# Eight sums and differences of w_out_b's weights, on GpSimd instead of VectorE

## The chip, the cores and the metric

The kernel runs on one core of one Trainium2 chip. The metric is the device time of one execution in microseconds; the time before is the median of three runs. The engines that matter here: TensorE (PE in the profile) multiplies, VectorE (DVE) and ScalarE (ACT) do elementwise work, GpSimd (POOL) does elementwise work and issues some DMAs, SyncE (SP) issues most DMAs. Each engine works through its own list of instructions in order; semaphores make an instruction wait for others.

## The reference

One inference step of a hybrid decoder layer, for a prompt of 1024 tokens and eight samples of one token (1032 columns together), model width 1024, all in float32. Cut to what matters:

```
proj = h @ w_in                       # h: normalised, modulated input
hA, cA, bA, zA, qkv, zB, beta, alpha, gA, gB = split(proj)
yA = ((bA * conv3(cA * hA)) * silu(zA)) @ w_out_a
o  = rmsnorm(gated_delta(qkv, beta, alpha)) * silu(zB)
yB = o @ w_out_b                      # (1032 x 1024) @ (1024 x 1024)
merged = sigmoid(gA) * yA + sigmoid(gB) * yB
y = x + gate * rmsnorm(merged @ w_o)
```

## The kernel before

The large matrix products are made from operands split in two: a float32 tile is cast to a TensorE format (hi, on ScalarE), the rest is taken by a subtraction (lo, on VectorE), and three matmuls hi*hi, hi*lo, lo*hi are summed in PSUM. A weight tile of 128 x 1024 becomes `whi` (ScalarE) and `wlo` (VectorE); each name has two buffers, so a new `whi` waits until TensorE has finished with the pair two units earlier.

The run has stages. After a startup, `run` makes the q, k, v, z and gate columns of `w_in` and, beside them, the gated delta rule of eight heads. Then `products` makes the four column blocks h, c, b, z of branch A (eight groups t of them), and `products_b` makes yB. Then `run` makes the products with `w_out_a`, and a tail those with `w_o`.

`products` and `products_b` use a scheme of seven products in place of eight (Strassen's, in Winograd's form). The matrix of weights is cut into quarters a11, a12, a21, a22, and four new quarters are made of them: s = a21 + a22, a21' = a11 - a21, a11' = s - a11, a12' = a12 - a11'. The seven products P1, P2, P6, P7, P4, P5, P3 (in this order) use a11, a12, a11', a21', a22, s, a12'. For yB there are two column groups g = 0, 1, and a unit is one product of one group: P1 of group 0 (P1.0), P1.1, P2.0, P2.1, P6.0 and so on. A unit is 48 matmuls.

`weight_load` (from line 1454) loads the raw quarters with SyncE into tiles named `wr`, in the order a11, a12, a21, a22, each for both groups; a load waits for a free tile. `weight_gen` (from line 1470) makes `whi` and `wlo` of one unit after another, and behind those of P2 the four new quarters of its group: s into a tile of its own, `wsum`, the others in place over the raw tiles. So a21' must wait for s (which reads a21), a11' for a21', for s and for P1's `wlo` (which reads a11), and a12' for a11' and P2's `wlo`. There are eight instructions of 128 x 1024 float32 for yB: two named `wsum<-wr`, two `wr<-wsum,wr`, four `wr<-wr`. The same four are made for each of the eight groups t of branch A.

`yblock_gen` (from line 1531) brings the moving operands of yB. For P1, P2 and P3 SyncE loads rows (`yraw<-yBsc`) that ScalarE and VectorE split into `thi` and `tlo`. For P6, P7, P4 and P5 ready-made halves were parked in DRAM (`txs`) by `park_gen`, and GpSimd issues their loads: four products x two pairs of rows x two parts, 16 DMAs. `finish_group` ends a group of branch A with elementwise work on tiles named `acc`; for the last group this falls into the first units of yB. `evacuate` adds a finished product into its tiles from PSUM, on VectorE, but for P1, which ScalarE copies.

The order of the work comes from strands (generators) that `slot` and `force` step through beside the matmuls, by the clocks of a planner, `Sched`. `Paced` charges each instruction to its engine's clock: a two-input VectorE instruction 66 ns + elements/0.96 (1133 ns for 1024), a GpSimd one 100 ns + elements/1.2 (953 ns for 1024). The framework below places the instructions anew on each engine; in the trace, sums stand ahead of products that the code writes before them.

Nearly all instructions carry the line of the helper that records them (L129), so the views are read by tile names.

Of the kernel before, what the change touches and what calls it, by code (L numbers as in the profile page):

```python
# [12 lines left out]
ALU = mybir.AluOpType  # L13
# [155 lines left out]
def hybrid_step(  # L169
# [9 lines left out]
    V, A, PE, GP, SY = (Paced(e, n, sched) for e, n in (  # L179
        (nc.vector, "V"), (nc.scalar, "A"), (nc.tensor, "PE"), (nc.gpsimd, "GP"), (nc.sync, "SY")))  # L180
# [12 lines left out]
    def tt(out, a, b, op):  # L193
        V.tensor_tensor(out=out, in0=a, in1=b, op=op)
# [495 lines left out]
    def when(*conds):  # L690
        while not all(c() for c in conds):
            yield
# [777 lines left out]
    def weight_gen(raw):  # L1470

        sums = {}
        for n, (key, p, g) in enumerate(UNITS):
            a11, a12, a21, a22 = ((key, o, hf, g) for o in range(2) for hf in range(2))
            src = {"P1": a11, "P2": a12, "P6": a11, "P7": a21, "P4": a22, "P5": None, "P3": a12}[p]
            yield from when(lambda: unit[0] >= n - 1, lambda: src is None or src in raw)
            hi_ = wpool.tile([P, NK, P], F32R, tag="whi", name="whi", bufs=2)
            lo_ = wpool.tile([P, NK, P], F32R, tag="wlo", name="wlo", bufs=2)
            hi, lo = (v.rearrange("p k c -> p (k c)") for v in (hi_, lo_))
            v = raw[src] if src else sums.pop(g)  # L1480
            A.copy(out=hi, in_=v)
            yield
            tt(lo, v, hi.bitcast(F32), ALU.subtract)
            made[key, p, g] = (hi_, lo_)
            yield
            if p == "P2":
                yield from when(lambda: a22 in raw and a21 in raw)
                s_ = wpool.tile([P, NK, P], F32, tag="wraw", name="wsum", bufs=2)
                s_ = sums[g] = s_.rearrange("p k c -> p (k c)")
                tt(s_, raw[a21], raw[a22], ALU.add)  # L1490
                yield
                tt(raw[a21], raw[a11], raw[a21], ALU.subtract)
                tt(raw[a11], s_, raw[a11], ALU.subtract)
                yield
                tt(raw[a12], raw[a12], raw[a11], ALU.subtract)
            elif p in ("P6", "P7", "P4", "P3"):
                T4.give(raw.pop(src))

# [238 lines left out]
    def to_products():  # L1737
        drain_bg()
        T4.free = [i for i in T4.free if i[0] is not bp]
        bp.release()  # L1740
        T4.extend(alloc("m", "left"), "sl", NSL, NT)
        EARLY.extend(("gate", "wr", "qa", "qb", "q1"))
        raw = {}
        for g in (weight_load(raw), weight_gen(raw), block_gen()):
            start(g)
# [136 lines left out]
    for j in range(9):  # L1882
# [7 lines left out]
        for half in range(2):  # L1890
# [20 lines left out]
            gt = gtp if i < 8 else gts  # L1911
# [5 lines left out]
        for half in range(2):  # L1917
            hs = slice(half * 512, (half + 1) * 512)
            stt(yt[:n, hs], yt[:n, hs], r, xr[:n, hs], ALU.mult, ALU.add)
            out = y_prompt[0, i * P:(i + 1) * P, hs] if i < 8 else y_sample[:, 0, hs]  # L1920
# [39 lines left out]
```

## Time and profile before

| what | value |
|---|---|
| median of 3 runs | 1376.41 us (1374.74 to 1377.12) |
| the profiled execution's own time | 1375.67 us |
| its span | 1373.2 us |
| mean granted TensorE clock | 0.997 |
| ScalarE, VectorE busy | 666.2 us (49%), 969.6 us (71%) |
| DMA moved | 165.99 MB, mean 121 GB/s |
| products of yB | units from 1088.9 us to about 1174 us |

Times in the views are microseconds from the start of the span. A row of the view in order of time gives start, duration, engine, operation, written tile, read tiles, shape and count; a bracket gives the idle time of the engine just before and what ended it. Durations of neighbours overlap a little, since an engine takes its next instruction before the last has drained; what one costs its engine is read from start to start. The chain that ended last is followed back from the last instruction, at each step to what released it. Matmul ends are modelled. Profiled time and span differ by 2.5 us, which lie around the span.

### The profile page before, as it was taken

The numbers are of one execution on the slowest core, as the hardware profiler recorded it, in microseconds if no ns is written. First come the engines' busy times: TensorE is split into PE (matmuls) and PEld (weight loads), VectorE is DVE, ScalarE is ACT, GpSimd is POOL, SyncE is SP. The second block draws the span as 40 slices with busy tenths as digits, with TensorE's granted clock in tenths as the row PEclk, the third lists the DMA queues.
The fourth block names the chain that finished last, engine by engine and source line by source line (L and its number), as shares of the span: only waits on it lengthen the run. The fifth ranks groups of instructions, "written<-read, shape, count | busy, mean of one in ns | idle before, by whom it ended". The sixth has DMA issues, their size and how long they took to land.

```text
span 1373.2 us, 26429 instructions
## 1 busy us (share of the span) xinstructions
PE 1342.7 (98%) x10257; PEld 1278.0 (93%) x10257; DVE 969.6 (71%) x2495; ACT 666.2 (49%) x1554; POOL 46.3 (3%) x98
## 2 busy tenths in 40 slices
PE   5999999999999999999999999999999999999997
PEld 2799999999999999999998999999999999999786
DVE  4677877686969576695755999777777777754553
ACT  5586685576757575564543543222333354431221
POOL 1000010000001000000000000000000300000000
PEclk9999999999999999999999999999999999999999
DMA  9433333333343234333431654422232956652221
GB/s 318 134 112 97 97 101 85 86 110 88 93 106 99 64 99 116 84 100 88 140 102 53 223 191 154 124 78 72 68 98 84 280 181 218 229 168 71 83 96 46
DMA packets 184927, 165.99 MB, mean 121 GB/s; under 512 B 33709, under 2 KB 158366, under 8 KB 184794
## 3 DMA queue, kind: packets, MB, share of 16 engines
q1 hardware_dynamic: 180216, 155.71, 37.3%
q0 software_dynamic: 4384, 8.52, 2.1%
q8 instruction: 81, 1.33, 0.4%
q14 instruction: 44, 0.36, 0.1%
q10 hardware_dynamic: 202, 0.08, 0.0%
HBM read 127.59 MB, written 36.91 MB: 120 GB/s over the span
## 4 chain that ended last, share of the span: by engine, by line
PE 84%; DVE 7%; ACT 4%; DMA 3%; issue 1%; SPq 0%; DVEq 0%; ACTq 0%
PE pm_t L129 58%; PE pa_t L129 24%; PE pb L129 3%; DVE kq L129 2%; DVE wlo L129 1%; ACT junk L129 1%; DMA xs<-in_x_prompt_dram 1%; DVE Ttmp L129 1%; DVE Ts L129 1%; DMA Ts<-sT 1%; DMA wr<-in_w_out_b_dram 1%; ACT whi L129 0%; SPq L129 0%; ACT DB L129 0%; DVE S L129 0%
## 5 line engine op out<-in xcount | busy, mean ns | idle before, releaser
L129 PE MATMUL pm_t<-xh,whi 128*128 128x344 f32 (+1 forms) x1384 | 453.0, 327 | 0.4 <-DVE ban L129 0.4
L129 PE MATMUL pm_t<-xh,wlo 128*128 128x344 f32 (+1 forms) x1384 | 434.0, 314 | 0.0
L129 PE MATMUL pm_t<-xl,whi 128*128 128x344 f32 (+1 forms) x1384 | 433.9, 313 | 0.0
L129 PEld LDWEIGHTS pm_t<-xh,whi 128*128 128x128 f32 x1384 | 261.1, 189 | 3.5 <-issue 1.2
L129 PEld LDWEIGHTS pm_t<-xl,whi 128*128 128x128 f32 x1384 | 261.1, 189 | 0.1
L129 PEld LDWEIGHTS pm_t<-xh,wlo 128*128 128x128 f32 x1384 | 260.4, 188 | 0.1
L129 ACT CAST whi<-wr 128x1024 fp32r<-128x1024 f32 x60 | 63.0, 1050 | 138.3 <-PE pa_t L129 61.7
L129 ACT CAST whi<-wraw 128x512 fp32r<-128x512 f32 x112 | 68.4, 626 | 61.4 <-PE pm_t L129 50.0
L129 DVE TENSOR_TENSOR wlo<-wraw,whi 128x512 fp32r<-128x512 f32 x112 | 75.8, 686 | 27.1 <-ACT whi L129 26.3
L129 PE MATMUL pm_t<-thi,wlo 128*128 128x258 f32 x304 | 86.7, 285 | 2.5 <-DVE wlo L129 2.5
L129 PE MATMUL pm_t<-tlo,whi 128*128 128x258 f32 x304 | 86.6, 285 | 0.0
L129 PE MATMUL pm_t<-thi,whi 128*128 128x258 f32 x304 | 86.4, 284 | 0.0
L129 PE MATMUL pa_t<-tlo,whi 128*128 128x258 f32 x304 | 85.9, 283 | 0.0
L129 PE MATMUL pa_t<-thi,wlo 128*128 128x258 f32 x304 | 85.8, 282 | 0.0
L129 PE MATMUL pa_t<-thi,whi 128*128 128x258 f32 x304 | 85.7, 282 | 0.0
L129 DVE TENSOR_TENSOR wlo<-wr,whi 128x1024 fp32r<-128x1024 f32 x60 | 73.2, 1220 | 11.3 <-ACT whi L129 11.0
L129 PE MATMUL pa_t<-xh,whi 128*128 128x258 f32 x256 | 72.4, 283 | 0.0
L129 PE MATMUL pa_t<-xl,whi 128*128 128x258 f32 x256 | 72.4, 283 | 0.0
L129 PE MATMUL pa_t<-xh,wlo 128*128 128x258 f32 x256 | 72.2, 282 | 0.0
L129 DVE SCALAR_TENSOR_TENSOR kq<-raw,vecs,kq 128x528 f32<-128x528 f32 x96 | 70.2, 759 | 1.1 <-ACT kq L129 1.1
L129 ACT ACT_TABLE_LOAD x42 | 53.9, 1283 | 27.1 <-DVE kq L129 12.8
L129 PE MATMUL pm_t<-yhi,wlo 128*128 128x344 f32 x192 | 61.4, 320 | 0.0
(377 smaller groups left out, 2954.3 us busy)
## 6 DMA issues: line engine op xcount, KB each, us to landing
wraw<-in_w_in_dram SPq DMA_DIRECT2D x48, 512.0 KB
wr<-in_w_in_dram SPq DMA_DIRECT2D x64, 256.0 KB
aw<-in_ada_w_dram SPq DMA_DIRECT2D x16, 512.0 KB
gBsc<-gate SPq DMA_DIRECT2D x8, 516.0 KB
gAsc<-gate SPq DMA_DIRECT2D x8, 516.0 KB
txs<-phi SPq DMA_DIRECT2D x8, 516.0 KB
txs<-plo SPq DMA_DIRECT2D x8, 516.0 KB
yAsc<-acc SPq DMA_DIRECT2D x8, 516.0 KB
```

The lines of the kernel that those rows point to most:

```text
L129: r = f(*args, **kw)
```

## The change

For the key "B", that is the weights of w_out_b, the four instructions that make the new quarters of a group are issued on GpSimd; for the eight groups of branch A they stay on VectorE. The instructions, their operands and their place in the code are the same. Nothing else is edited; the planner charges them to GpSimd's clock.

```diff
                 s_ = wpool.tile([P, NK, P], F32, tag="wraw", name="wsum", bufs=2)
                 s_ = sums[g] = s_.rearrange("p k c -> p (k c)")
-                tt(s_, raw[a21], raw[a22], ALU.add)
-                yield
-                tt(raw[a21], raw[a11], raw[a21], ALU.subtract)
-                tt(raw[a11], s_, raw[a11], ALU.subtract)
-                yield
-                tt(raw[a12], raw[a12], raw[a11], ALU.subtract)
+                gt = tt if key != "B" else lambda o, a, b, op: GP.tensor_tensor(out=o, in0=a, in1=b, op=op)
+                gt(s_, raw[a21], raw[a22], ALU.add)
+                yield
+                gt(raw[a21], raw[a11], raw[a21], ALU.subtract)
+                gt(raw[a11], s_, raw[a11], ALU.subtract)
+                yield
+                gt(raw[a12], raw[a12], raw[a11], ALU.subtract)
```

## The prediction

> **What bounds the kernel now.** I read the page first, then the chain that ended last around the products of yB, then TensorE's and VectorE's instructions at the one break in that chain. (P1.0, P1.1, P2.0 and so on are product and column group g of the yB units; a11, a12, a21, a22 are their raw weights; s is the tile wsum.)
>
> ```profile
> span 1373.2 us, 26429 instructions
> PE 1342.7 (98%) x10257; PEld 1278.0 (93%) x10257; DVE 969.6 (71%) x2495; ACT 666.2 (49%) x1554; POOL 46.3 (3%) x98
> ```
>
> TensorE is busy 98% of the span and GpSimd 3%. Time off VectorE pays only where TensorE waits for VectorE. The chain shows one such place near the change (start us, us, what):
>
> ```profile
> 1077.49 1.06 ACT whi L129
> 1078.58 1.24 DVE wlo L129
> ...
> 1079.83 0.37 SPq L129
> ...
> 1080.25 8.46 DMA wr<-in_w_out_b_dram
> ...
> 1088.73 0.04 DVE wsum L129
> ...
> 1091.82 7.31 PE pm_t L129 x46
> 1099.12 5.72 PE pa_t L129 x48
> 1104.84 5.74 PE pm_t L129 x48
> 1110.58 5.75 PE pa_t L129 x48
> ...
> 1180.79 184.57 PE pm_t L129 x974
> ```
>
> To the right of 1091.82 the chain is TensorE alone to 1365, one unit of 48 matmuls every 5.75 us in the products of yB. To the left it leaves TensorE: a load of w_out_b takes 8.46 us, and a sum (wsum) starts when it lands. TensorE in order of time at that place:
>
> ```profile
> 1088.94 0.28 PE L129 MATMUL pm_t<-thi,whi 128*128 128x258 f32 x1
> 1089.06 0.28 PE L129 MATMUL pm_t<-tlo,whi 128*128 128x258 f32 x1
> 1091.82 0.58 PE L129 MATMUL pm_t<-thi,wlo 128*128 128x258 f32 x1 [2.48 <-DVE wlo L129]
> 1092.19 0.42 PE L129 MATMUL pm_t<-thi,whi 128*128 128x258 f32 x1
> ...
> 1095.21 0.31 PE L129 MATMUL pm_t<-thi,wlo 128*128 128x258 f32 x1
> ```
>
> P1.0 starts at 1088.94, issues two matmuls 0.12 us apart, and then stands until wlo, the low part of its weights. After that it runs at about half speed for 3.4 us; the view by stretches gives the granted clock (third figure from the end of a row, 0.59 and 1.00; before it busy time and instructions of each engine):
>
> ```profile
> 1092.00:1096.00 4.00, 4.00 (x22) 4.00 (x23) 4.00 (x9) 1.26 (x2) 2.46 (x4) 0.59 1.22 353
> 1096.00:1110.00 14.00, 14.00 (x120) 14.00 (x119) 13.22 (x15) 8.82 (x21) 0.00 (x0) 1.00 0.96 311
> ```
>
> Why wlo was late is in VectorE's and ScalarE's order of time (the bracket is the idle time before the instruction and what ended it):
>
> ```profile
> 1083.25 1.05 ACT L129 CAST whi<-wr 128x1024 fp32r<-128x1024 f32 x1 [4.71 <-PE pm_t L129]
> ```
> ```profile
> 1081.92 0.76 DVE L129 TENSOR_TENSOR acc<-pm_t,acc 128x258 f32<-128x258 f32 x2 [0.67 <-PE pm_t L129]
> 1088.73 1.22 DVE L129 TENSOR_TENSOR wsum<-wr 128x1024 f32<-128x1024 f32 x1 [6.05 <-DMA wr<-in_w_out_b_dram]
> 1089.88 0.75 DVE L129 TENSOR_TENSOR acc<-pm_t,acc 128x258 f32<-128x258 f32 x2
> 1090.55 1.22 DVE L129 TENSOR_TENSOR wlo<-wr,whi 128x1024 fp32r<-128x1024 f32 x1
> ...
> 1103.79 1.22 DVE L129 TENSOR_TENSOR wr<-wr 128x1024 f32<-128x1024 f32 x1
> 1104.92 1.22 DVE L129 TENSOR_TENSOR wr<-wsum,wr 128x1024 f32<-128x1024 f32 x1
> ...
> 1108.06 1.22 DVE L129 TENSOR_TENSOR wlo<-wr,whi 128x1024 fp32r<-128x1024 f32 x1 [0.78 <-ACT whi L129]
> ```
>
> whi of P1.0 was ready at 1084.3. Its wlo needs nothing else, but on VectorE it stands behind wsum of group 1, which waits 6.05 us for the last raw tile (a22 of group 1). The sum itself is used only by P5, many units later. An early, unneeded instruction holds up a late, needed one.
>
> **The change part by part.** *What leaves VectorE.* Eight instructions; between 1074 and 1112 us the view by tile lists exactly these:
>
> ```profile
> L129 DVE TENSOR_TENSOR wr<-wr x4: 1212/1216/1217, 1076.8 to 1109.5; 128x1024 f32<-128x1024 f32 x4
> L129 DVE TENSOR_TENSOR wsum<-wr x2: 1211/1218/1224, 1075.3 to 1088.7; 128x1024 f32<-128x1024 f32 x2
> L129 DVE TENSOR_TENSOR wr<-wsum,wr x2: 1214/1215/1216, 1092.3 to 1104.9; 128x1024 f32<-128x1024 f32 x2
> ```
>
> One costs VectorE 1.13 us, by start to start (1103.79 to 1104.92): 8 x 1.13 = 9.0 us. By itself this is worth nothing, since TensorE is the bound. What pays is the wait that leaves with wsum: VectorE no longer idles until 1088.73. wlo of P1.0 can follow its cast and the two evacuations queued before it: 1084.3 + 0.7 + 1.2, about 1086.2, which is 2.7 us before P1.0 starts.
>
> *The gain.* The third matmul of P1.0 would start 0.12 us after the second, at 1089.18 instead of 1091.82: 2.64 us. From 1091.82 to 1095.21 there are 16 intervals; at 0.12 us they take 1.92 instead of 3.39: 1.47 us. I take the half clock as the consequence of the break, as it is granted 0.59 there and 1.00 behind it. Together **4.1 us**. Nothing later in the chain is there to give it back: up to 1365 it holds only matmuls.
>
> *What GpSimd takes on.* No two-input arithmetic on GpSimd stands in the trace. The nearest rows are its copies (min/median/max in ns), and one of them beside VectorE:
>
> ```profile
> L129 POOL COPY raw<-hist_q x24: 205/208/2813, 63.6 to 578.1; 128x24 f32<-128x24 f32 x24
> ```
> ```profile
> L129 POOL COPY Ts<-Ti x8: 402/403/1152, 118.1 to 642.4; 128x256 f32<-128x256 f32 x8
> ```
> ```profile
> 187.69 2.81 POOL L129 COPY raw<-hist_q 128x24 f32<-128x24 f32 x1 [15.27 <-DVE kq L129]
> ```
> ```profile
> 187.49 0.67 DVE L129 TENSOR_TENSOR wlo<-wraw,whi 128x512 fp32r<-128x512 f32 x1
> 188.09 1.21 DVE L129 TENSOR_TENSOR kq<-kq,gcB 128x1024 f32<-128x1024 f32 x1
> 189.23 1.21 DVE L129 TENSOR_TENSOR DB<-DA,m_strict 128x1024 f32<-128x1024 f32 x1
> ```
>
> The undisturbed copies give 0.85 ns an element ((402 - 205) / 232), so a 1024-element copy would take 1.05 us: the lower bound. A second input read one after the other adds 0.87: **1.92 us**, my value, as it is the copy rows' own slope. Eight separate 256-element copies, 3.2 us, are the upper bound. The Trainium skill's GPSIMD Engine Reference, section 3.1 (Elementwise, side-by-side cycle accounting), gives 4497 ns for a two-input add of 2048 elements; an estimate of half, 2.25 us, lies inside these bounds.
>
> The copy at 187.69 takes 2.81 us instead of 0.21 and ends at 190.50, just as VectorE's three back-to-back two-input instructions end (189.23 + 1.21 = 190.44). So the two engines shut each other out for something. The trace shows GpSimd waiting, up to 2.6 us; whether VectorE waits for a long GpSimd instruction no row here can show, since GpSimd's own ones are too short. I bound it by 0 and by the whole GpSimd instruction. The Trainium skill's SBUF — State Buffer, section "Who interferes with whom", says that a VectorE instruction with two SBUF inputs and a GpSimd instruction that reads SBUF contend for an exclusive lock, and that whoever starts first holds it for the whole instruction. By that rule VectorE would wait; the stretched copy agrees with its other half.
>
> *What this does to VectorE.* Before, five of the eight sums run from 1088.73 up to wlo of P2.1 (1108.06), and that wlo ends 1.3 us before its unit (1109.3 against 1110.58): the tightest deadline. After, VectorE is free 5.3 us earlier (1083.4 instead of 1088.7) and TensorE 4.1 us earlier, a head start of 1.2 us. If each of the five kept VectorE shut out for all its 1.92 us, the lag would be 5 x (1.92 - 1.13) = 4.0 us, against 1.3 + 1.2 = 2.5 of room: wlo 1.5 us late. If half of that time falls on idle time or on evacuations, whose one input is in PSUM, the lag is 2.0 or less and nothing is late. VectorE has evacuations in every unit and no longer has the sums, so I take the half: cost **0**, bounds 0 and 5 x (3.2 - 1.13) - 2.5 = 7.9 us.
>
> *GpSimd's queue.* It also issues the loads of the parked blocks:
>
> ```profile
> 1089.51 0.71 POOL L129 DMA_DIRECT2D tlo<-txs  x1 [9.53 <-PE pa_t L129]
> ```
> ```profile
> thi<-txs POOLq DMA_DIRECT2D x8, 516.0 KB, 6.7
> ```
>
> Sums and these issues now stand in one line. A load put behind wsum of group 1 leaves up to 1.9 us after the tile's landing at 1088.7 and still lands some 7 us later, about 1098; the first block needed is P6's, loaded first, by unit four (1088.94 + 4 x 5.75 = 1111.9). Cost 0; cover gone if an issue slips by over 10 us. The other way round, sums behind the issues: seven more of 0.71 us after 1089.51 end near 1094.5; the sums s and a11' that P6.0's cast needs by 1106.2 (when P2.1 starts and a weight buffer is free) come second there, 1094.5 + 2 x (1.92 + 2.6) = 1103.5. Covered by 2.7 us. The planner charges GpSimd 953 ns for such an instruction and VectorE 1133, so the strands behind may be placed differently. I cannot price that from the trace; it widens the range.
>
> **The sum.** The profiled execution took 1375.67 us (span 1373.2 and 2.5 around it): 1375.67 - 4.1 = 1371.6. The median of the three runs lies 0.74 above it, so on that level the forecast is 1376.41 - 4.1 = **1372.3 us**.
>
> **The rivals.** *Eaten by the shared access.* Up to five GpSimd sums keep VectorE out for all their time; wlo of P2.1 is 1.5 us late, and with a fresh half-clock stretch of 1.5 us the kernel takes 1372.3 + 3.0 = 1375.3: no change. For it: VectorE is busy through 13.22 of 14 us at 1096 to 1110. Against: GpSimd is the one seen waiting. With the skill's price of 2.25 us in the same sum, wlo would be 3.1 us late and the time 1376.9.
>
> *The wait stays.* Another early instruction, waiting for the same loads, is placed before wlo of P1.0, or the raw tile comes later: 1376.4. For it: VectorE's order in the trace is not the code's (wsum ran ahead of a product that the code writes earlier), so it is newly made. Against: the other instructions in reach, evacuations and finish_group, follow TensorE and not a load.
>
> *Slower: GpSimd holds VectorE out.* The same place, wlo of P2.1, with a dearer instruction. Lateness is 5 x (p - 1.13) - 2.5, and 1.5 for the clock; it exceeds the gain of 4.1 and 0.2% (2.75) from p = 2.7 us on. At the upper bound of 3.2: 1372.3 + 7.9 + 1.5 = 1381.7. For it: the copy rows are single-input and say little of two inputs; against: their slope is far below, and TensorE would have to catch all five.
>
> **How the numbers follow.** A measurement of this kernel can tell about 0.2% (2.75 us) from no change: faster is below 1373.66, slower above 1379.16. Forecast, full gain or nearly: 50%, its own range 1370.8 to 1373.6. Eaten 18%, the wait stays 10%: 28% within 0.2%. Slower 22%. The range runs from 1370.8 (the forecast less 1.5 for the spread of runs, 1374.74 to 1377.12 before) up to 1380, leaving out the dearest of the slower cases, some 15%, and a few per cent below.
>
> **What would show it.** Right: no wait for wlo at P1.0, no stretch with a clock near 0.59 behind it, the eight sums on GpSimd near 1.9 us where VectorE is quiet, and wlo of P2.1 ahead of its unit. VectorE's two-input instructions of 128x1024 should stay at 1.2 us if it is not shut out; at 2 to 3 us they show the lock. Wrong: a new wait for wlo between P1.1 and P6.1, for whi behind a late a11', or for a parked block; or the DMA wait found again on VectorE before P1.0. A GpSimd sum above 2.7 us on its own would overturn the forecast.

## The result and the profile after

The changed kernel takes **1385.01 us** (median of six runs, 1382.53 to 1387.8) against 1375.68 us for the kernel before in six runs of its own (1374.56 to 1377.12). The ratio is **1.0067, interval 1.0053 to 1.0081**: 9.3 us slower. The forecast was 1372.3 us, and the time lies above its range, which ended at 1380.

The top of the page after, span and busy times:

```profile
span 1383.5 us, 26449 instructions
PE 1346.2 (97%) x10257; PEld 1279.7 (93%) x10257; DVE 973.5 (70%) x2487; ACT 665.8 (48%) x1554; POOL 66.5 (5%) x106
```

VectorE has eight instructions fewer (2487 for 2495), and yet its busy time has gone up, from 969.6 to 973.5 us. Eight instructions of 1.2 us left, and something else grew by more than they took. That is the first sign of where to look.

TensorE in order of time; the view shows no other wait of over 0.3 us from 1087 to the end:

```profile
1106.40 0.58 PE L129 MATMUL pm_t<-thi,wlo 128*128 128x258 f32 x1 [5.04 <-DVE wlo L129]
```
```profile
1121.58 0.39 PE L129 MATMUL pm_t<-thi,whi 128*128 128x258 f32 x1 [2.30 <-ACT whi L129]
1122.84 0.39 PE L129 MATMUL pm_t<-thi,wlo 128*128 128x258 f32 x1 [0.75 <-DVE wlo L129]
```

The wait of 2.48 us at P1.0 is gone. In its place stand 5.04 us at P2.0 (for VectorE) and 2.30 + 0.75 us at P6.0 (for ScalarE, then VectorE). Counting 48 matmuls to a unit gives each unit's start in both traces, and the shift of after against before tells what each place costs:

| unit | before, us | after, us | shift, us | step, us |
|---|---|---|---|---|
| P1.0 | 1088.94 | 1089.37 | +0.43 | |
| P1.1 | 1098.96 | 1095.16 | -3.80 | -4.23: the old wait and its half clock |
| P2.0 | 1104.68 | 1100.96 | -3.72 | +0.08 |
| P2.1 | 1110.42 | 1113.36 | +2.94 | +6.66: first new wait |
| P6.0 | 1116.17 | 1121.58 | +5.41 | +2.47: second new wait |
| P6.1 | 1121.91 | 1129.97 | +8.06 | +2.65: its second half, and the clock |
| first unit of w_out_a | 1173.77 | 1181.84 | +8.07 | 0.01 |
| last matmul | 1364.95 | 1374.85 | +9.90 | +1.83: in the stages behind yB |

So the forecast gain was made to the tenth of a microsecond (4.23), and then lost more than three times over: 6.7 us at P2.0, 5.1 us at P6.0, 1.8 us behind. In this trace both waits also leave a stretch at a lower granted clock (third figure from the end), here behind the second:

```profile
1123.00:1127.00 4.00, 4.00 (x22) 4.00 (x23) 3.73 (x7) 0.43 (x1) 0.00 (x0) 0.57 0.24 52
```

**The first new wait.** VectorE in order of time, from the sums of group 1 to wlo of P2.0:

```profile
1091.13 3.10 DVE L129 TENSOR_TENSOR wlo<-wr,whi 128x1024 fp32r<-128x1024 f32 x1
1094.15 2.37 DVE L129 SCALAR_TENSOR_TENSOR acc<-hist_a,vecs,acc 128x8 f32<-128x8 f32 x1
1096.44 3.50 DVE L129 SCALAR_TENSOR_TENSOR acc<-acc,vecs 128x1022 f32<-128x1022 f32 x1
1099.85 2.82 DVE L129 SCALAR_TENSOR_TENSOR acc<-hist_a,vecs,acc 128x8 f32<-128x8 f32 x1
1102.71 2.50 DVE L129 TENSOR_TENSOR acc<-acc 128x1032 f32<-128x1032 f32 x2
1105.13 1.22 DVE L129 TENSOR_TENSOR wlo<-wr,whi 128x1024 fp32r<-128x1024 f32 x1
```

and GpSimd beside it:

```profile
1090.64 2.50 POOL L129 TENSOR_TENSOR wsum<-wr 128x1024 f32<-128x1024 f32 x1 [7.26 <-DMA wr<-in_w_out_b_dram]
...
1093.84 2.64 POOL L129 TENSOR_TENSOR wr<-wsum,wr 128x1024 f32<-128x1024 f32 x1
1096.44 2.41 POOL L129 TENSOR_TENSOR wr<-wr 128x1024 f32<-128x1024 f32 x1
...
1100.26 2.39 POOL L129 TENSOR_TENSOR wr<-wsum,wr 128x1024 f32<-128x1024 f32 x1
```

The same two instructions of 128x8 in the trace of before:

```profile
1097.76 0.22 DVE L129 SCALAR_TENSOR_TENSOR acc<-hist_a,vecs,acc 128x8 f32<-128x8 f32 x1
...
1099.09 0.22 DVE L129 SCALAR_TENSOR_TENSOR acc<-hist_a,vecs,acc 128x8 f32<-128x8 f32 x1
```

An instruction of 0.22 us takes 2.37 us: it ends at 1096.52, just as the GpSimd sum begun at 1093.84 ends (1096.48). The next one, of 1.27 us, takes 3.50 beside the sum at 1096.44, and the second 128x8 one 2.82, until 1102.67, where the sum at 1100.26 ends (1102.65). In these rows the engines take turns: one VectorE instruction for each whole GpSimd sum. The row at 1091.13 is stretched too, beside wsum. These four and wlo of P2.0 are the trap: wlo, due at 1101, comes at 1105.13, behind all of finish_group. In before it stands ahead of the last `acc<-acc`; here behind both.

**The second new wait.** The chain that ended last, where it leaves TensorE (start us, us, what):

```profile
1105.24 6.92 DMA yAsc<-acc
...
1112.60 6.90 DMA yraw<-yBsc
...
1119.53 0.04 ACT thi L129
...
1120.49 1.05 ACT whi L129
```

and ScalarE in order of time:

```profile
1118.19 1.05 ACT L129 CAST yhi<-yraw 128x1032 fp32r<-128x1032 f32 x1 [8.66 <-DMA yraw<-yAsc]
1119.53 1.05 ACT L129 CAST thi<-yraw 128x1032 fp32r<-128x1032 f32 x1 [0.29 <-DMA yraw<-yBsc]
1120.49 1.99 ACT L129 CAST whi<-wr 128x1024 fp32r<-128x1024 f32 x2
```

finish_group ends late (1105.2), so its store `yAsc<-acc` starts at 1105.24. That is only 1.3 us later than before (1103.90); the larger part of the delay is the order on SyncE. Its rows behind the store, in before and then in after:

```profile
1104.88 0.36 SPq L129 DMA_DIRECT2D yraw<-yBsc  x1
1106.76 0.88 SPq L129 DMA_DIRECT2D yraw<-yAsc  x2
```
```profile
1112.18 0.33 SPq L129 DMA_DIRECT2D yraw<-yAsc  x1
1112.60 0.54 SPq L129 DMA_DIRECT2D yraw<-yBsc  x1
```

Before, the row of yB is asked for 1 us after the store. After, a row for w_out_a (`yraw<-yAsc`) stands between them and waits until the store has landed, 6.9 us (before, the first such row went out 2.9 us after the store), and the row of yB goes out behind it at 1112.60. ScalarE has the casts of those rows, which are for P3 and for the products with w_out_a much later, ahead of whi of P6.0, and idles 8.66 us for a row that nobody needs yet. It is the old pattern on another engine: an early instruction fed by a DMA holds up a needed one.

### The profile page after: what moved, and what is told of

It is laid out like the page before. It is cut to its first block, busy times and chain, and to the rows that moved or that the text cites. A ratio compares the mean times of both kernels' runs of the same rounds, so it can differ in the third digit from the quotient of the medians.

```text
span 1383.5 us, 26449 instructions
## 1 busy us (share of the span) xinstructions
PE 1346.2 (97%) x10257; PEld 1279.7 (93%) x10257; DVE 973.5 (70%) x2487; ACT 665.8 (48%) x1554; POOL 66.5 (5%) x106
## 4 chain that ended last, share of the span: by engine, by line
PE 80%; DVE 10%; DMA 5%; ACT 3%; issue 1%; SPq 1%; DVEq 0%; ACTq 0%
PE pm_t L129 54%; PE pa_t L129 23%; PE pb L129 3%; DVE kq L129 2%; DVE wlo L129 1%; DMA Ts<-sT 1%; DVE Ttmp L129 1%; DVE Ts L129 1%; DVE acc L129 1%; SPq L129 1%; DMA xs<-in_x_prompt_dram 1%; ACT junk L129 1%; DVE vT L129 1%; DVE S L129 1%; DMA rg_r<-in_ada_w_dram 1%
## 5 line engine op out<-in xcount | busy, mean ns | idle before, releaser
L129 DVE TENSOR_TENSOR wlo<-wr,whi 128x1024 fp32r<-128x1024 f32 x60 | 76.6, 1277 | 13.0 <-ACT whi L129 12.8
L129 PEld LDWEIGHTS pm_t<-thi,wlo 128*128 128x128 f32 x304 | 58.9, 194 | 6.2 <-DVE wlo L129 6.2
```

Of the source, the lines that this page charges most:

```text
L129: r = f(*args, **kw)
```

## The experiments

The theories: the loss is made by GpSimd holding VectorE out (its sums, at P2.0), against a worse placement by the planner, which now charges another clock; and the second wait follows from the first, against a limit of its own, that of rows whose casts stand ahead of needed ones, or of the loads as a whole, where another row takes the place of the one moved. Each ratio is against the kernel before on the same chip.

**The engine or the planner?** The change does two things: it moves the sums, and it charges them to another clock of the planner. The first kernel keeps the sums on VectorE and charges GpSimd; the second does the reverse. The edits of this and the next two parts are shown against the changed kernel.

```diff
-                gt = tt if key != "B" else lambda o, a, b, op: GP.tensor_tensor(out=o, in0=a, in1=b, op=op)
+                def gt(o, a, b, op, key=key):
+                    if key != "B":
+                        return tt(o, a, b, op)
+                    nc.vector.tensor_tensor(out=o, in0=a, in1=b, op=op)
+                    sched.note("GP", 100.0 + D / 1.2)
```

> The eight sums stay on VectorE; only the planner's charge for them goes to GpSimd's clock, as in the changed kernel. Theory L (GpSimd's sums shut VectorE out of SBUF while they run, 2.4 us each): no VectorE instruction of 128x8 to 128x1032 in the first units of yB is over 1.3 us, P2.0 has no 5 us wait, and the time is within 4 us of before (1375.7). Theory P (the planner's other charge places strands, slots and loads differently, and that is what costs): near the changed kernel, 1382 to 1386, with waits of TensorE at P2.0 and P6.0 as there. A mixed result, a wait of 2 to 4 us at P2.1 or P6.0 behind a late yraw load and none at P2.0, would give 1377 to 1380: the first wait is the lock's, the second the planner's.

Measured: 1375.78 us, ratio 1.0002 (0.9993 to 1.0012). A wait of 3.20 us at P1.0 stays.

```diff
...
+                    nc.gpsimd.tensor_tensor(out=o, in0=a, in1=b, op=op)
+                    sched.note("V", 66.0 + D / 0.96)
```

> The eight sums run on GpSimd, but the planner charges VectorE as before the change, so strands and slots come as before. Theory L: VectorE's two-input instructions beside a sum still take 2.4 us or more, wlo of P2.0 or P2.1 is 3 us or more late, and the time is 1378 or more. Theory P: the forecast gain of 4.1 us appears whole, 1371 to 1373.

Measured: 1385.18 us, 1.0067 (1.0052 to 1.0082), with both new waits:

```profile
1105.46 0.58 PE L129 MATMUL pm_t<-thi,wlo 128*128 128x258 f32 x1 [5.16 <-DVE wlo L129]
```

The planner's charge is worth nothing that these runs can tell, either way; the engine is worth all of the 9 us. The order on SyncE goes with the engine too: in the first kernel the row of yB stands ahead of the rows for w_out_a, in the second behind two of them.

**Is it the length of the GpSimd instruction?** A copy in place of the sum is less than half as long and reads one input (the second is left out); the order on the other four engines is that of the changed kernel, instruction for instruction.

```diff
...
+                    nc.gpsimd.tensor_copy(out=o, in_=a if o is not a else b)
+                    sched.note("GP", 100.0 + D / 1.2)
```

> In place of each of the eight sums GpSimd copies one of its inputs (the second input is left out); VectorE, ScalarE, SyncE and TensorE have the changed kernel's order of instructions throughout. Theory L: what VectorE loses per instruction is GpSimd's own duration, so with a copy of 1.1 us in place of a sum of 2.4 us the lag shrinks by more than half: no stretched VectorE instruction over 2.4 us, a wait at P2.0 of less than 1 us instead of 5.0, and 1371 to 1377. Theory P (order): the order is the changed kernel's, so the time stays at 1382 or more.

Measured: 1374.43 us, 0.9993 (0.9984 to 1.0003). The yB units gain 4.22 us at P1.0, no wait follows at P2.0, and 0.76 us at P6.0. VectorE's rows, with the one stretched instruction first, and the GpSimd copy beside it:

```profile
1094.70 1.00 DVE L129 SCALAR_TENSOR_TENSOR acc<-hist_a,vecs,acc 128x8 f32<-128x8 f32 x1
1095.73 2.50 DVE L129 TENSOR_TENSOR acc<-acc 128x1032 f32<-128x1032 f32 x2
1098.15 1.21 DVE L129 TENSOR_TENSOR wlo<-wr,whi 128x1024 fp32r<-128x1024 f32 x1
```
```profile
1093.58 2.10 POOL L1493 COPY wr<-wsum 128x1024 f32<-128x1024 f32 x1 [1.11 <-DVE acc L129]
1099.49 1.04 POOL L1493 COPY wr<-wr 128x1024 f32<-128x1024 f32 x1 [1.74 <-issue]
```

Here wlo of P2.0 starts at 1098.15, some 7 us earlier than in the changed kernel, and is done before its unit starts (1102.07). So the order that put it behind finish_group is not enough to make the wait; the time that GpSimd holds VectorE is. The taking of turns goes on: the copy of 1.04 us takes 2.10 while VectorE works, then VectorE waits for it. The length is not all that differs, though. The copy of a21 into s does not wait for the last raw tile, so the copies are spread out: from 1091 to 1103 us there are two of them, where the changed kernel has four sums. How much of the difference is the length and how much the crowding is not shown. Since the order is the same, the second wait can be compared as well: 3.05 us in the changed kernel, 0.76 here.

**Reading or only being busy?** GpSimd fills the tile twice in place of the sum, which is left out (two instructions of 0.96 us that read nothing).

```diff
...
+                    for _ in range(2):
+                        nc.gpsimd.memset(o, 0.01)
+                    sched.note("GP", 100.0 + D / 1.2)
```

> In place of each of the eight sums GpSimd fills the same tile twice with a constant, writing and not reading (the sums are left out). Theory L, as the Trainium skill's page SBUF — State Buffer words it (a two-input VectorE instruction contends with a GpSimd instruction that reads SBUF, not with one that only writes): VectorE's 128x8 instructions beside a fill stay at 0.2 to 0.3 us, its 128x1024 ones at 1.2 to 1.3 us, and TensorE has no wait over 1 us at P2.0: 1371 to 1376. If any work of GpSimd shuts VectorE out, those instructions are stretched to 1 us and 2 us beside a fill, as beside the copies, and a wait of 1 us or more comes at P2.0.

Measured: 1372.85 us, 0.9980 (0.9971 to 0.9989), the fastest of all: yB is 3.0 us shorter. Its time is no target, since a fill of s waits for no load; what counts are the rows. The fills on GpSimd and VectorE beside them:

```profile
1092.64 0.96 POOL L1494 MEMSET wr<- 128x1024 f32 x1 [1.04 <-DVE wlo L129]
1094.25 0.98 POOL L1494 MEMSET wr<- 128x1024 f32 x1
```
```profile
1092.50 0.22 DVE L129 SCALAR_TENSOR_TENSOR acc<-hist_a,vecs,acc 128x8 f32<-128x8 f32 x1
1092.64 1.27 DVE L129 SCALAR_TENSOR_TENSOR acc<-acc,vecs 128x1022 f32<-128x1022 f32 x1
1093.83 0.22 DVE L129 SCALAR_TENSOR_TENSOR acc<-hist_a,vecs,acc 128x8 f32<-128x8 f32 x1
1094.09 2.50 DVE L129 TENSOR_TENSOR acc<-acc 128x1032 f32<-128x1032 f32 x2
```

Every VectorE instruction has the duration of before, though GpSimd is busy beside the long ones. It is the GpSimd instruction that reads SBUF which shuts VectorE out. The Trainium skill's SBUF — State Buffer, section "Who interferes with whom", says that a VectorE instruction with two SBUF inputs contends with a GpSimd instruction that reads SBUF and not with one that only writes it. The trace agrees: the 128x1022 instruction takes 1.27 us beside a fill and 3.50 beside a sum.

**Is one moved sum enough?** The old wait came from one instruction alone, s of group 1. The edit is shown against the kernel before.

```diff
+                gs = tt if (key, g) != ("B", 1) else lambda o, a, b, op: GP.tensor_tensor(out=o, in0=a, in1=b, op=op)
-                tt(s_, raw[a21], raw[a22], ALU.add)
+                gs(s_, raw[a21], raw[a22], ALU.add)
```

> Only s of group 1, the one instruction that made VectorE wait for a load, goes to GpSimd; the other seven stay on VectorE. Theory L: one shut-out of 2.4 us where TensorE has room, the wait at P1.0 gone: 1371.5 to 1374. VectorE's a21' of group 1 now waits for GpSimd's s, to about 1091, and wlo of P1.1 stands behind it, so up to 1 us of the gain may go there. Theory P: the planner's clocks change for one instruction only and nothing else moves: 1371.5 to 1373 as well; this run does not tell the two apart, it shows whether the forecast gain can be had without the other seven.

Measured: 1375.87 us, 1.0003 (0.9995 to 1.0012). From P1.0 to P1.1 TensorE gains 4.2 us, all of the forecast gain; then P2.1 waits, and it is gone (+1.28 at P2.1, +2.64 in the unit behind):

```profile
1108.05 0.39 PE L129 MATMUL pa_t<-thi,whi 128*128 128x258 f32 x1 [0.81 <-ACT whi L129]
1109.31 0.39 PE L129 MATMUL pa_t<-thi,wlo 128*128 128x258 f32 x1 [0.75 <-DVE wlo L129]
```

ScalarE in this kernel, and then in the kernel before:

```profile
1104.90 1.06 ACT L129 CAST thi<-yraw 128x1032 fp32r<-128x1032 f32 x1 [6.29 <-DMA yraw<-yBsc]
...
1106.92 1.08 ACT L129 CAST whi<-wr 128x1024 fp32r<-128x1024 f32 x1
```
```profile
1104.93 1.06 ACT L129 CAST thi<-yraw 128x1032 fp32r<-128x1032 f32 x1 [3.69 <-DMA yraw<-yBsc]
...
1106.95 1.08 ACT L129 CAST whi<-wr 128x1024 fp32r<-128x1024 f32 x1
```

TensorE is 3.7 us ahead, and the row lands at the same moment (1104.90 and 1104.93), although its load was issued 1.3 us earlier (1097.92 and 1099.24): it does not come sooner because TensorE is sooner. whi of P2.1 stands behind it. In before that left 1.1 us of room (whi at 1106.95, then wlo, 1109.3, against the unit's start at 1110.42); a gain of 4.1 us uses it up and waits for the rest. A second limit lay hardly a microsecond behind the first.

**Can those casts be moved away?** Rows are loaded when a tile is free. The next kernels give the rows of P3 the tile that was freed last, so that their load, and the cast behind it, come later.

```diff
-        def get(self, name, w):
-            i = min((i for i in self.free if i[2] >= w),
+        def get(self, name, w, late=False):
+            i = min((i for i in (self.free[::-1] if late else self.free) if i[2] >= w),
...
-                    raw, hi, lo = (T4.get(n_, NT) for n_ in ("yraw", "thi", "tlo"))
+                    raw, hi, lo = (T4.get(n_, NT, p == "P3") for n_ in ("yraw", "thi", "tlo"))
```

On the kernel with the one sum moved:

> As the run with only s of group 1 on GpSimd, and the rows of P3, which are loaded and cast 50 us before their use, are given the tiles that came free last, so their casts stand far behind the weights of P2.1 and P6.0 on ScalarE. Theory H (the forecast gain came at P1.0 and was given back at P2.1 because ScalarE casts those rows, late from DMA, ahead of whi): the waits at P2.1 and P6.0 go, the gain of 4.2 us stays, 1370.5 to 1373. Theory D (the loads as a whole are at their limit there, whatever their order): another load takes their place in front of whi and TensorE waits 2 us or more again, 1375 to 1377.

Measured: 1374.64 us, 0.9989 (0.9980 to 0.9998): between the two ranges, and the best kernel that does all the work, 0.1% better than before. Its yB is 1.3 us shorter than in before (83.51 against 84.83). Waits of 0.64 us (P1.1) and 0.29 + 0.76 us (P2.1) took the rest of the gain. At P1.1 wlo stands behind a21' of group 1, which waits on VectorE for s from GpSimd; ahead of whi of P2.1 there now stands the cast of another row, for w_out_a.

On the kernel before:

> The kernel before with the rows of P3 held back in the same way, nothing on GpSimd. Theory H: the wait at P1.0 stays (2.5 to 3.2 us and half clock), nothing else was late before, so 1374.5 to 1377, no change. If holding back alone makes it 1373 or less, H is wrong about what the holding does.

Measured: 1376.52 us, 1.0005 (0.9996 to 1.0013), with 2.32 us of waiting at P1.0: by itself the edit does nothing to the time. Its yB is as short as that of the kernel above, 83.58 us, because no lower clock follows its wait (see the last section); its P1.0 starts 1.8 us later than in before, so yB ends no sooner. So what speaks for the kernel above is its whole time, not its yB.

On the changed kernel:

> The changed kernel with the rows of P3 held back. Theory L with H: the first wait (about 5 us before wlo of P2.0, plus half clock, made by the lock) stays; the second one (2.3 + 0.75 us before whi and wlo of P6.0, behind the late rows) goes or shrinks below 1 us: 1380 to 1383. If the rows were the cause of both, 1375 or less; if the second wait is the lock's too, 1384 to 1386.

Measured: 1383.39 us, 1.0061 (1.0045 to 1.0077). Both waits stay (5.06, and 2.21 + 0.75 us), the second again behind a cast of a row for w_out_a, and a gate. Other early work has taken the place of the row moved.

**All rows late.** The same edit on the rows of w_out_a and the gate as well tests whether the second wait is made by these casts and apart from the first.

```diff
+        sg = T4.get("sg", NT, True)
...
+            raw, hi, lo = (T4.get(n_, NT, True) for n_ in ("yraw", "yhi", "ylo"))
```

> The changed kernel with all three kinds of work that is loaded early and used late (rows of P3, rows of yA, gates) given the tiles that came free last. Theory L with H: the first wait, about 5 us before wlo of P2.0 plus half clock, is the lock's and stays; the second, before whi of P6.0, comes from the late store of branch A's last group, the rows behind that store, and their casts in front of whi on ScalarE; with those casts moved back it goes: 1378.5 to 1381.5. If the second wait is the lock's directly (wlo or a11' late), 1383 or more.

Measured: 1389.04 us, 1.0095 (1.0079 to 1.011). In yB only the first wait is left,

```profile
1106.18 0.58 PE L129 MATMUL pm_t<-thi,wlo 128*128 128x258 f32 x1 [5.37 <-DVE wlo L129]
```

and from P2.1 to P3.1 the shift against before stays at 3.5 us, where the changed kernel goes on from 2.9 to 8.1. So the second wait needs these casts and can be removed without the first; it is worth 5.1 us. It is not independent of the first: with the same order and no first wait, the kernel with copies kept 0.76 us of it. The whole kernel is slower because the rows are now late for w_out_a, which waits 1.15, 1.30 and 3.43 us for yhi.

> The kernel before with the same three kinds of work held back, nothing on GpSimd. The wait at P1.0 (2.3 to 3.2 us and half clock) is not touched: 1375 to 1377, no change. If the held-back rows and gates come too late for the products with w_out_a, 1378 or more; if they alone were what bound yB, 1373 or less.

Measured: 1387.91 us, 1.0090 (1.0076 to 1.0104): waits for yhi in the stage behind on the old kernel too (the longest 2.94 and 1.97 us); the edit itself costs them.

**Without GpSimd.** Another order of the sums needs no s at the start: a21' = a11 - a21 in the extra tile, a11' = a22 - a21', and s = a21 + a22 only after P4. All stay on VectorE, and the first one waits for a21, not for the last tile (`b_` is true for the weights of w_out_b).

```diff
+                if b_:
+                    tt(s_, raw[a11], raw[a21], ALU.subtract)
+                    yield
+                    tt(raw[a11], raw[a22], s_, ALU.subtract)
+                    yield
+                    tt(raw[a12], raw[a12], raw[a11], ALU.subtract)
...
+            elif b_ and p == "P4":
+                tt(raw[a22], raw[a21], raw[a22], ALU.add)
```

> All eight on VectorE in the order that cannot wait early for the last raw tile; no load is held back. If casts of early rows in front of whi give the gain back, P1.0 has no wait, a wait of 1 to 2.5 us stands at P2.1 or P6.0 behind a cast that waited for its load, and the time is 1374 to 1377. If nothing gives it back here: 1371 to 1373.

Measured: 1376.38 us, 1.0006 (0.9997 to 1.0014). No wait from P1.0 to P2.1; then 0.52 + 1.28 us at P6.0, and yB takes 84.5 us against 84.8 before. The cast ahead of whi:

```profile
1111.52 1.05 ACT L129 CAST thi<-yraw 128x1032 fp32r<-128x1032 f32 x1 [6.78 <-DMA yraw<-yBsc]
1112.48 1.04 ACT L129 CAST whi<-wr 128x1024 fp32r<-128x1024 f32 x1
```

With P3's rows late:

> All eight on VectorE, none on GpSimd, written so that none can stand early on VectorE waiting for the last raw tile: a21' goes into the extra tile, a11' = a22 - a21' into a11 (after P1's wlo), s = a21 + a22 into a22 after P4's wlo. Rows of P3 held back. If the one early instruction was the cause of the wait at P1.0 and the lock the cause of the loss, this has the gain without the loss: 1370.5 to 1373, no wait of TensorE above 0.5 us in yB. If VectorE's load of sums matters by itself, waits for wlo come back at P2.0 or P2.1 and it is 1374 or more.

Measured: 1376.89 us, 1.0010 (1.0001 to 1.0019): yB is 2.4 us shorter, one wait of 1.27 us is left at P6.0, behind the cast of a row for w_out_a, and the stages behind lose 2.3.

With all rows late:

> All eight on VectorE in the order that cannot wait early for the last raw tile, and all three kinds of early work held back. If the wait at P1.0 and the casts in front of whi are all that keeps TensorE waiting in yB, the forecast gain of 4.1 us is whole here: 1370.5 to 1373, no wait of TensorE above 0.5 us in yB. If something else is next (VectorE's own load, or the loads as a whole), a wait appears at another unit and it is 1374 to 1377.

Measured: 1382.89 us, 1.0051 (1.0038 to 1.0064). yB runs without any wait, 80.58 us against 84.83: **4.25 us, the forecast gain, kept to the end of yB.** Behind it TensorE waits for the late rows:

```profile
1178.64 0.42 PE L129 MATMUL pm_t<-yhi,whi 128*128 128x344 f32 x1 [1.12 <-ACT yhi L129]
1190.64 1.51 PE L129 MATMUL pm_t<-yhi,whi 128*128 128x344 f32 x4 [2.98 <-ACT yhi L129]
1196.94 1.26 PE L129 MATMUL pm_t<-yhi,whi 128*128 128x344 f32 x4 [2.63 <-ACT yhi L129]
```

With P3's rows and the gate late, those of w_out_a on time:

> The same with the rows of P3 and the gates held back and the rows of yA on time. If the casts in front of whi were the cause: no wait over 0.8 us in yB, none over 1 us in the products with w_out_a, 1371 to 1373.5. If the loads as a whole are at their limit: waits of 1 us or more in either place, 1374.5 to 1378.

Measured: 1379.16 us, 1.0029 (1.0019 to 1.0039): waits of 0.80 + 1.63 us at P6.0 behind the cast of a row for w_out_a, and 1.38 us in the stage behind.

> The kernel before with the rows of P3 and the gates held back: control. The wait at P1.0 stays, so the time is 1374.5 to 1377; if the moved loads alone bring it to 1373.5 or less, the wait at P1.0 was not what bound yB.

Measured: 1377.68 us, 1.0016 (1.0007 to 1.0025): 3.74 us at P1.0 stay (in the profiled execution, which at 1381.33 us was the longest of eleven).

These six kernels with one sum moved or with the new order say the same thing: as long as some rows come early, yB gives part or all of its gain back, for the most part at a cast ahead of whi, and if all come late, the stage behind waits. Loads of w_out_b, of the parked blocks and of the rows share the same stretch; in the kernel without waits in yB the DMA engines were busy 0.94 of the time from 1090 to 1120 us (second figure from the end), in before, second row, 0.79:

```profile
1090.00:1120.00 30.00, 30.00 (x252) 30.00 (x251) 19.14 (x27) 14.57 (x26) 4.95 (x7) 1.00 0.94 317
```
```profile
1090.00:1120.00 30.00, 28.18 (x223) 28.18 (x224) 27.91 (x39) 16.83 (x28) 4.46 (x7) 0.94 0.79 245
```

That the loads as a whole are the limit here is suggested by these runs and not shown: other loads than before stand in that stretch.

## Why the prediction was wrong

- **The gain at P1.0** was right in mechanism, and in size for the execution that was read: forecast 4.1 us, measured 4.23, and 4.2 wherever the sum of group 1 leaves VectorE's path, always against the one profiled execution of before. (From 1091.82 to 1095.21 the view has 15 intervals, not 16; with 15 the forecast's own sum gives 4.23.) The 1.6 us of it that are the lower clock are partly luck: such a stretch does not follow every wait, as the last section shows.
- **What GpSimd takes for a sum** was too low: 2.38 to 2.41 us when undisturbed, against the 1.92 that I took. The copies' slope held for a copy (1.04 against 1.05 forecast), but a second input more than doubles it. The estimate of 2.25 us, half of the 4497 ns that the Trainium skill's GPSIMD Engine Reference, section 3.1, gives for 2048 elements, was nearer.
- **The cost of the shared access is the step that failed first**: "If half of that time falls on idle time or on evacuations [...] the lag is 2.0 or less and nothing is late." It fell on neither. From 1091.13 to 1102.71 VectorE ran four instructions that take 1.13 + 0.14 + 1.19 + 0.14 = 2.6 us by start to start in before (2.7 beside the fills), and took 11.6 us for them. The half was a choice without a row behind it: with the measured 2.4 us and no halving the step's own sum gives 5 x (2.4 - 1.13) - 2.5, some 3.9 us late. The sum of the step charged each GpSimd sum with its own length less VectorE's saving; the right one charges each VectorE instruction that meets it, however small, with a wait of up to one whole sum. I had counted the sums, and not the instructions that meet them. So it caught P2.0, a unit ahead of the place I named. The two rivals that named this mechanism had the cause right; both had the place (P2.1) wrong, and the size too: 1375.3 us, and 1381.7 at the upper bound, against 1385.0. The slower one should have decided from p = 2.7 us on, and 2.4 sufficed.
- **"Nothing later in the chain is there to give it back" failed as well**, on its own, as the kernel with one moved sum shows: seven sums stay on VectorE, nothing shuts it out for long, and the gain is lost all the same; so it is with the new order and no sum on GpSimd. The chain shows only what ended last. What would end last next stood in ScalarE's rows that I quoted nowhere: a cast that waited 3.69 us for a load, 1.1 us ahead of being the bound. I had seen the room (as 1.3 us, against the chain's 1110.58; the unit starts at 1110.42), put it down to VectorE's load alone, and added a "head start" that the landing of this load did not give.
- **GpSimd's queue** at nothing: TensorE never waits for a parked block in the trace after. **The planner**, left without a price: nothing, by the two kernels that charge the other clock.
- **The rival that the wait stays** was wrong: no wait for wlo at P1.0.
- **That s is used only by P5** was a misreading: a11' reads s as well, and P6 uses a11'. It changes nothing at P1.0, but with s of group 1 alone on GpSimd VectorE's a21' stands 3.17 us until that s is done.

Open: the 1.8 us behind yB in the changed kernel were not tested by themselves (with P3's rows late they do not show). Whether a placement of the loads exists that keeps all 4.1 us is open too; the best found is about 1 us faster than before.

## What to carry to other kernels

A wait on the chain of what ended last is worth only as much as the room up to the next limit: before pricing its removal, go through every in-order engine for instructions fed by a DMA that stand ahead of needed ones, and do not count on their loads to land sooner. Work moved to GpSimd beside a busy VectorE was not priced here by its elements, but by the number of VectorE instructions with two SBUF inputs that met it, times up to one whole GpSimd instruction; four of them cost 9.0 us. Fewer and shorter copies of 1.04 us made no wait at P2.0, where the sums of 2.4 us made one of 5 us. An instruction that waits for a load is best ordered behind what is needed sooner, or made from operands that land earlier; here that took the wait away, and the next limit kept the time.

## What was not expected of the hardware

- A two-input GpSimd sum of 128x1024 takes 2.4 us, 2.3 times the copy of the same size (1.04). Where VectorE works on two inputs it grows as well; the first sum takes 3.08 us:

```profile
1074.34 3.08 POOL L129 TENSOR_TENSOR wsum<-wr 128x1024 f32<-128x1024 f32 x1 [1.20 <-DMA wr<-in_w_out_b_dram]
```

- Not all of VectorE is shut out. During that first sum two evacuations with one input in PSUM keep their 0.76 us:

```profile
1075.08 0.76 DVE L129 TENSOR_TENSOR acc<-pa_t,acc 128x258 f32<-128x258 f32 x2
```

- Short waits of TensorE can be enough for the lower clock. In the kernel with one moved sum the waits are 0.81 + 0.75 us, and the 4 us behind them have a mean granted clock of 0.57 (third figure from the end). The two units lose 3.92 us (1.28 + 2.64), 2.4 more than the waits; in the changed kernel the second wait, 3.05 us in two pieces, costs 5.12.

```profile
1109.50:1113.50 4.00, 4.00 (x22) 4.00 (x22) 4.00 (x8) 2.60 (x4) 0.00 (x0) 0.57 0.42 168
```

- But the lower clock does not follow every wait. In the kernel before with P3's rows late, TensorE waits 2.32 us at P1.0, and behind it the full clock is granted:

```profile
1094.00:1098.00 4.00, 4.00 (x35) 4.00 (x35) 4.00 (x8) 1.27 (x2) 2.27 (x4) 1.00 1.22 363
```

P1.0 takes 8.39 us there, 2.6 more than the 5.79 us without a wait (in after), where in before a wait of 2.48 us costs 4.23. So two profiles of yB can differ by 1.6 us and more by this alone, and a difference of that size between them is not yet a gain. What decides whether the clock is lowered is not shown by these runs.
